# Where a step of layer 1's attention empties its accumulator bank: directly behind the value products, or at the end of the step

## The chip, the cores and the metric

The kernel runs on one core of one Trainium2 chip. The metric is device time in microseconds of one execution, taken as the median over runs. The engines carry their short names of the profile: PE is TensorE's matrix products (PEld its weight loads), DVE is VectorE, ACT is ScalarE, POOL is GpSimd, SP is SyncE, which issues the DMAs.

## What is computed

One inference step of a two-layer streaming encoder, over 2048 prompt frames and 64 sample frames of width 1024. Layer 0 has latent attention and banded attention. Layer 1, the one that matters here, is grouped-query attention in a sliding window: 16 query heads share 2 key/value heads of 64 dimensions, a chunk of 64 frames reads itself and the two chunks before it, and each head has a learned sink that joins the softmax's sum. The output is gated, projected and normalised:

```python
def _c_layer(h, pos, cache, pre_g, post_g, w_in, sinks, w_out):
    b, s, _ = h.shape
    xn = _rms(h, pre_g)
    q, k, v, g = _split(xn @ w_in, C_SIZES)
    ...
    if cache is None:
        o = _band_prompt(q, k, v, C_PAST_CHUNKS, C_SCALE, sinks=sinks)
    ...
    return h + _rms((o * jax.nn.silu(g)) @ w_out, post_g), state
```

## The kernel before

The kernel runs five phases one after the other. Phases 1 to 4 are layer 0 and the input projection of layer 1. Phase 5, which the change touches, is layer 1's attention together with its output projection, and it takes about the last 440 us. In all matrix products a number is split into a high and a low part, so a value operand has 128 columns: 64 of the high part and 64 of the low part.

**Units and blocks.** The prompt's 2048 queries are 16 blocks of 128, worked in the order 8 to 15, then 0 to 7 (`BLOCKS5`). A block has four units, one for each of two key/value heads `g` and each of two halves `e` of that head's query heads. A unit is four heads by 128 queries, against 256 keys in two tiles of 128. Block 0 has one tile of keys only (`nb` is 1), since nothing precedes it; it is the ninth block worked.

**Steps.** The loop over steps (`step`, line 1897) is a pipeline over units written out by hand. Step n exponentiates unit n+1 (line 1717, ACT), issues the scores of unit n+2 (line 1705, PE, with four row maxima on DVE, line 1708), turns the probabilities of unit n by transposes, and multiplies the turned probabilities of unit n-1, called `prv`, by its values. The last two go over the two key tiles, b = 0 and b = 1:

- `turn` (line 1723): four transposes into a bank `t` of PSUM (line 1726), and a copy of the high part into `PT` on ACT (line 211, a helper).
- `pump(RATE5 / 2)`: some products of the output projection of an older block (line 964). Now and then a half of a projected tile is finished; then ACT copies it to `z` (line 211) and squares it (line 983).
- `low()`: the low part of `PT`, on DVE (line 214, a helper), which reads the same bank `t`.
- at b = 0 only, `prv.av()` (line 1808): the value products of the previous unit, four matrix products (two for block 0) into the accumulator `acc`, line 1733.

**Evacuation.** After both tiles the step calls `prv.out()` (line 1813). ACT copies the low-part half of the accumulator to `tbm` (line 1822, shown as line 211), and DVE adds the other half to it and writes the block's output tile `OT` (line 1823). For the first unit of a block, (g, e) = (0, 0), `out` must first open a new `OT`. While two blocks are open it calls `J.rest()` and `pump(1)` until one of them is closed (lines 1816 to 1818). For the last unit, (1, 1), it also takes the reciprocal of the sums (line 1827) and hands the block to `gate`.

**Side work.** `J.rest()`, called at the end of every step and in that loop, moves several generators on by one stage. One is `gate` (line 1735): it spreads the reciprocals over the partitions by transposes (line 1755), multiplies `OT` by them on DVE (line 1757) and by the gate on POOL (line 1763), copies the result to `MM` on ACT (line 211), closes the block, and has POOL make the low part of `MM` (line 1770). Another is the tail of the output projection: a chain of small instructions for the root mean square, two multiplications `z` on DVE (line 995), the residual addition `x` on POOL (line 1003), and the store.

**Order.** From the ninth step on (`NAUTO5` is 8), PE, DVE, ACT and SP execute in the order in which the program names the instructions. POOL's order is left to the scheduler of the framework, and in the first eight steps so is that of all engines. Each engine works its queue in order.

**Space.** PSUM has 8 banks: two score tiles of two banks each, two banks `t` for transposes, one bank `acc` for value products, one bank `proj` for the projection. `OT` and `tbm` have two buffers each.

Of the kernel before, what the change touches and what calls it, by code (L numbers as in the profile page):

```python
# [110 lines left out]
def kernel(ctx, tc, a, o, upto=5):  # L111
# [1555 lines left out]
    def phase5():  # L1667

        with ExitStack() as st:
# [213 lines left out]
            def pump(rate):  # L1883
                if J.mm:
                    return J.pump(rate)
                for _ in range(RATEL):
                    if next(left, left) is left:
                        return open_projections()
# [8 lines left out]
            def step(n):  # L1897
                cur, prv, nxt = us.get(n), us.get(n - 1), us.get(n + 1)
                if nxt:
                    nxt.exp([0, 1, 2, 3])  # L1900
                if n + 2 < len(units):
                    us[n + 2] = Unit(*units[n + 2])
                    us[n + 2].start()
                    if n % 4 == 1 and n // 4 + 2 < 16:
                        blocks[n // 4 + 2] = Block(BLOCKS5[n // 4 + 2])
                for b in range(2):
                    low = None
                    if cur and b < cur.B.nb:
                        PT, low = cur.turn(b * 128, 128)
                        cur.tasks.append(PT)  # L1910
                    pump(RATE5 / 2)
                    if low:
                        low()
                    if b == 0 and prv:
                        prv.av()
                if prv:
                    prv.out()
                    us.pop(n - 1)
                    if n % 4 == 0 and n // 4 + 1 in blocks and n > 0:
                        blocks[n // 4 + 1].load_values()  # L1920
                if not J.loaded:
                    J.load.pump(1)
                if n >= NS5:
                    J.samp.pump(1)
                if J.made < FAST5:
                    J.side.pump(SP5)
                J.rest()

            for n in range(NAUTO5):
                step(n)  # L1930
            with manual(M5, ORDERED | {mybir.EngineType.SP}):
                for n in range(NAUTO5, len(units) + 1):
                    step(n)
                J.banks += [(ps_t, "t"), (ps_o, "acc")]
                J.dense = True
                while J.done < 17:
                    J.side.pump(TAIL)
                    J.samp.pump(1)
                    J.rest()
                    J.last = J.done == 16  # L1940
                    J.pump(4)
                J.side.drain()
                J.tails.drain()
# [104 lines left out]
```

## Time and profile before

| quantity | value |
|---|---|
| median of 3 runs | 2689.81 us (2688.68 to 2691.74) |
| the profiled execution, its own time | 2687.59 us |
| its span in the profile | 2685.8 us |
| granted TensorE clock, mean | 0.988 |
| PE busy | 2562.0 us (95%) |
| PEld busy | 2337.2 us (87%) |
| DVE busy | 1568.8 us (58%) |
| ACT busy | 1391.8 us (52%) |
| POOL busy | 520.5 us (19%) |
| DMA | 437.94 MB, mean 163 GB/s |

Times in the profile are microseconds from the start of the span. A row of a timeline gives the start, the time taken, the engine, the line of the kernel, the operation, the tile written and the tile read, their shapes and how many instructions the row merges. A bracket at its end gives the idle time of the engine just before and what ended it. The busy shares are means over the whole kernel; phase 5 has its own balance, which the prediction reads.

### The profile page before, as it was taken

Reading aid. Unit: us, or ns where it says so; the run is one execution under the profiler, and the core shown is the slowest. Engines: PE = TensorE matmul, PEld = TensorE weight load, DVE = VectorE, ACT = ScalarE, POOL = GpSimd, SP = SyncE. Lnnn points to the kernel's source line nnn. Section 1 sums busy time; section 2 is a strip of 40 time slices with the busy share of each in tenths; the row PEclk is TensorE's granted clock in tenths of the full one; section 3 lists DMA queues with packets and bytes.
Section 4 is the critical chain, followed back from the end, with each engine's and each line's share of the span. In section 5 each row is a group of like instructions: output and inputs, shape, how many; then the busy total and the mean of one; then the engine's idle time right before and its main releaser. Section 6 shows DMA issues by size and latency. Waiting matters only on the chain.

```text
span 2685.8 us, 46771 instructions
## 1 busy us (share of the span) xinstructions
PE 2562.0 (95%) x16296; PEld 2337.2 (87%) x16296; DVE 1568.8 (58%) x4299; ACT 1391.8 (52%) x3548; POOL 520.5 (19%) x1110
## 2 busy tenths in 40 slices
PE   7999999999999999999999999899999998999997
PEld 6999999899998888888778888689999998787886
DVE  6553345453227878787668776575224214787886
ACT  4332242322327777777667666553223214877773
POOL 0001000001002333221200323432001000344443
PEclk9999999999999999999999999999999999999999
DMA  7546343737537666661387776666525328555552
GB/s 243 170 152 210 124 149 113 246 111 220 173 94 201 190 180 185 175 188 49 114 243 188 201 201 177 176 233 230 152 84 176 122 72 249 118 142 135 132 133 71
DMA packets 382283, 437.94 MB, mean 163 GB/s; under 512 B 49936, under 2 KB 308888, under 8 KB 378816
## 3 DMA queue, kind: packets, MB, share of 16 engines
q1 hardware_dynamic: 382048, 434.95, 55.2%
q8 instruction: 130, 2.13, 0.3%
q14 instruction: 105, 0.86, 0.1%
HBM read 282.80 MB, written 157.09 MB: 164 GB/s over the span
## 4 chain that ended last, share of the span: by engine, by line
PE 79%; DVE 9%; ACT 5%; DMA 3%; issue 3%; POOL 1%; SPq 0%; ACTq 0%; DVEq 0%; POOLq 0%
PE pm L237 39%; PE proj L964 10%; PE s L683 6%; PE acc L754 4%; PE t L726 3%; PE acc L1228 3%; DVE PT L214 2%; PE s L1176 2%; PE t L1203 2%; PE t L1726 2%; PE acc L1733 2%; PE s L1705 1%; ACT P L702 1%; DVE m L689 1%; DVE s L1708 1%
## 5 line engine op out<-in xcount | busy, mean ns | idle before, releaser
L237 PE MATMUL pm<-X,W 128*128 128x384 f32 (+2 forms) x4536 | 754.3, 325 | 2.1 <-DVE ev L214 1.6
L237 PEld LDWEIGHTS pm<-X,W 128*128 128x128 f32 x4536 | 732.0, 189 | 5.3 <-DVE ev L214 1.9
L211 ACT ACTIVATE PT<-t 128x512 fp32r<-128x512 f32 (+3 forms) x704 | 344.1, 505 | 265.4 <-PE t L1203 76.2
L214 DVE SCALAR_TENSOR_TENSOR PT<-t,PT 128x512 fp32r<-128x512 f32 (+3 forms) x688 | 377.2, 569 | 91.6 <-ACT PT L211 89.0
L964 PE MATMUL proj<-Wo,MM 128*128 128x512 f32 (+1 forms) x1416 | 389.8, 406 | 5.0 <-ACT z L211 3.1
L214 DVE SCALAR_TENSOR_TENSOR ev<-pm,ev 128x256 fp32r<-128x256 f32 (+3 forms) x197 | 98.6, 503 | 336.0 <-ACT ev L430 101.2
L964 PEld LDWEIGHTS proj<-Wo,MM 128*128 128x128 f32 (+1 forms) x1416 | 245.2, 186 | 51.9 <-ACT z L211 6.5
L237 PE MATMUL pm<-W,X 128*128 128x256 f32 (+5 forms) x2040 | 281.2, 297 | 0.0
L237 PEld LDWEIGHTS pm<-W,X 128*128 128x128 f32 (+1 forms) x2040 | 272.0, 187 | 1.0
L702 ACT ACTIVATE P<-s,m 128x512 f32<-128x512 f32 (+9 forms) x344 | 209.5, 616 | 33.1 <-DVE m L691 30.5
L683 PE MATMUL s<-KA,Q 128*128 128x512 f32 (+7 forms) x640 | 201.4, 397 | 9.4 <-ACT P L702 8.4
L228 DVE TENSOR_TENSOR W<-R,W 128x768 fp32r<-128x768 f32 (+3 forms) x114 | 116.1, 1055 | 133.5 <-ACT W L227 133.1
L726 PE MATMUL t<-ident,P 128*128 128x128 f32 x1088 | 176.4, 276 | 3.4 <-ACT P L702 0.8
L689 DVE TENSOR_REDUCE m<-s 128x1 f32<-128x480 f32 (+7 forms) x216 | 132.4, 613 | 80.5 <-PE s L683 80.1
L726 PEld LDWEIGHTS t<-ident,P 128*128 128x128 f32 x1088 | 134.6, 141 | 41.6 <-ACT P L702 15.1
L754 PE MATMUL acc<-PT,V 128*128 128x256 f32 x1152 | 156.0, 285 | 6.5 <-DVE OT L763 6.5
L754 PEld LDWEIGHTS acc<-PT,V 128*128 128x128 f32 x1152 | 140.4, 188 | 12.0 <-PE t L726 6.0
L1717 ACT ACTIVATE P<-s,m 128x256 f32<-128x256 f32 (+2 forms) x264 | 119.6, 466 | 10.7 <-DVE m L1709 9.4
L1708 DVE CUSTOM_DVE_ANT_0 s<-s,mask 128x256 f32<-128x256 f32 (+1 forms) x256 | 107.6, 422 | 18.5 <-PE t L1726 7.7
L1228 PE MATMUL acc<-PT,V 128*128 128x256 f32 x672 | 111.5, 298 | 6.7 <-DVE OT L1238 4.5
L683 PE MATMUL s<-KR,Q 128*128 128x384 f32 (+6 forms) x320 | 116.3, 363 | 1.1 <-DMA Q<-sQR 1.1
L1180 DVE CUSTOM_DVE_ANT_0 s<-s,bias 128x640 f32<-128x640 f32 (+4 forms) x128 | 95.2, 744 | 35.1 <-PE s L1176 33.5
(251 smaller groups left out, 3941.2 us busy)
## 6 DMA issues: line engine op xcount, KB each, us to landing
Q<-sQA SPq DMA_DIRECT2D x128, 128.0 KB, 3.3
sWO<-W SPq DMA_DIRECT2D x32, 512.0 KB, 3.8
Q<-sQB SPq DMA_DIRECT2D x128, 128.0 KB, 3.3
Wo<-sWO SPq DMA_DIRECT2D x16, 1024.0 KB, 9.1
Q<-sQC SPq DMA_DIRECT2D x32, 512.0 KB, 7.2
R<-in_ab_w_in_dram SPq DMA_DIRECT2D x40, 384.0 KB, 4.0
K<-sKB SPq DMA_DIRECT2D x56, 256.0 KB, 5.4
V<-sVB SPq DMA_DIRECT2D x24, 512.0 KB, 6.3
```

What stands on the lines that cost most here:

```text
L211: nc.scalar.activation(out, in_, AF.Copy)
L214: nc.vector.scalar_tensor_tensor(out, x, scale, hi, op0=ALU.mult, op1=ALU.subtract)
L237: nc.tensor.matmul(ps, lhs(x, k), rhs(y, k), start=(j == 0), stop=(j == n - 1))
L683: nc.tensor.matmul(s[:r, :n], self.Q[:, x, self.qo:self.qo + r], rhs, start=(x == 0), stop=(x == 2))
L689: nc.vector.tensor_reduce(m[:r, j:j + 1], s[:r, :n], axis=AX.X, op=ALU.max)
L702: nc.scalar.activation(self.P[:r, o0:o0 + n], self.s.pop(j)[:r, :n], AF.Exp, bias=self.m[:r, 6:7], accum_out=acc)
L726: nc.tensor.transpose(t[:, b], self.P[:, (b0 + b) * 128:(b0 + b + 1) * 128], ident)
L754: nc.tensor.matmul(acc[:, (i // 2) % 2], H.V[:, b0 + b], PT[:, x, b], start=(b0 + b == 0 and x == 0), stop=(b0 + b == i and x == 1))
L964: nc.tensor.matmul(p, M[:, x, k, :r], W[k][:, y, cs], start=(k == k0 and t == 0), stop=(k == k1 - 1 and t == 2))
L1228: nc.tensor.matmul(acc, self.H.V[:, self.base - self.H.b0 + b], self.PT[:, x, off + b], start=(b == 0 and x == 0), stop=(b == nblk - 1 and ...
L1708: nc.vector.tensor_tensor_reduce(s[:, c, :w], s[:, c, :w], mk, 1.0, -3e38, ALU.add, ALU.max, m[:, 0, c:c + 1])
L1717: nc.scalar.activation(self.P[:, c, :w], self.s[:, c, :w], AF.Exp, bias=m[:, 1, c:c + 1], accum_out=m[:, 0, c:c + 1])
```

## The change

The call of `prv.out()` moves from behind the loop over the two key tiles into it, directly behind `prv.av()` at b = 0. With it move the copy to `tbm`, the addition, for a block's first unit the loop that runs side work and projection products until a block is closed, and for its last unit the reciprocal. What followed it in the step stays where it was.

```diff
                     if b == 0 and prv:
                         prv.av()
+                        prv.out()
                 if prv:
-                    prv.out()
                     us.pop(n - 1)
                     if n % 4 == 0 and n // 4 + 1 in blocks and n > 0:
                         blocks[n // 4 + 1].load_values()
```

## The prediction

> **What bounds the kernel now.** I read the page first, then the busy time by stretches, then the waits of the last 440 us (layer 1's attention with its output projection), then the timeline of single engines there.
>
> ```profile
> span 2685.8 us, 46771 instructions
> ```
>
> The busy time of two stretches follows. The columns are the stretch, its length, busy time of PE, PEld, DVE, ACT and POOL, granted clock, DMA share and GB/s.
>
> ```profile
> 2260.00:2300.00 40.00, 32.66 (x182) 23.42 (x181) 32.72 (x112) 30.48 (x99) 7.10 (x22) 0.96 0.64 177
> 2500.00:2550.00 50.00, 48.27 (x283) 40.98 (x283) 43.56 (x112) 39.64 (x118) 22.76 (x50) 1.00 0.57 139
> ```
>
> In the settled part TensorE is busy 48.27 of 50 us at full clock, VectorE 43.56. So TensorE sets the pace, and only its idle time, here 1.7 us in 50, can be won. The stretch from 2260 is looser: 7.3 us idle in 40. Who waits for whom from 2245 to the end (us in total, times, longest):
>
> ```profile
> DVE OT L1823 <- ACT tbm L211: 16.4, 28, 3.6
> PE acc L1733 <- DVE OT L1823: 13.9, 16, 3.8
> ```
>
> The value products wait 13.9 us for the addition that empties their only accumulator bank, by far TensorE's largest wait in this stage. TensorE's timeline shows where; the number in brackets is the idle time ahead of the row.
>
> ```profile
> 2363.72 1.17 PE L1733 MATMUL acc<-PT,VC 128*128 128x512 f32 x4 [0.58 <-DVE OT L1823]
> ...
> 2462.43 0.73 PE L1733 MATMUL acc<-PT,VC 128*128 128x512 f32 x2 [3.85 <-DVE OT L1823]
> ...
> 2607.49 1.16 PE L1733 MATMUL acc<-PT,VC 128*128 128x512 f32 x4 [0.71 <-DVE OT L1823]
> ...
> 2631.84 1.16 PE L1733 MATMUL acc<-PT,VC 128*128 128x512 f32 x4 [1.65 <-DVE OT L1823]
> ```
>
> From 2363.72 to 2607.49 there are ten such waits of 0.58 to 0.81 us, one in each block of four units (24.35 us apart when settled), together 7.2 us. Beside them stands one of 3.85, at the block that has a single tile of keys, and one of 1.65 at the end. The remaining 1.2 us lies in small ones, mostly before 2340, and I count nothing for it.
>
> Next, one settled block on four engines. I call three steps A, B and C. A's value products are those at 2399.74, and it evacuates the last unit of a block. B's are at 2405.27, and it evacuates the first unit of the next. C's are at 2412.39, and they stall.
>
> ```profile
> 2399.74 0.63 PE L1733 MATMUL acc<-PT,VC 128*128 128x512 f32 x2
> ...
> 2402.73 0.60 PE L1726 MATMUL t<-ident,P 128*128 128x128 f32 x4
> ...
> 2405.27 1.09 PE L1733 MATMUL acc<-PT,VC 128*128 128x512 f32 x4
> 2406.20 0.60 PE L1726 MATMUL t<-ident,P 128*128 128x128 f32 x4
> 2406.56 3.01 PE L964 MATMUL proj<-Wo,MM 128*128 128x512 f32 x12
> ...
> 2412.39 1.17 PE L1733 MATMUL acc<-PT,VC 128*128 128x512 f32 x4 [0.74 <-DVE OT L1823]
> ...
> 2415.07 0.66 PE L1726 MATMUL t<-ident,P 128*128 128x128 f32 x4
> ```
>
> ```profile
> 2400.84 0.60 ACT L211 ACTIVATE PT<-t 128x512 fp32r<-128x512 f32 x1 [2.11 <-PE t L1726]
> 2401.54 0.60 ACT L211 ACTIVATE z<-proj 128x512 f32<-128x512 f32 x1
> 2402.16 0.59 ACT L211 ACTIVATE tbm<-acc 64x512 f32<-64x512 f32 x1
> ...
> 2405.69 0.21 ACT L983 ACTIVATION_READ_ACCUMULATOR sq<-z 128x1 f32 x1
> 2406.84 0.60 ACT L211 ACTIVATE PT<-t 128x512 fp32r<-128x512 f32 x1 [0.93 <-PE t L1726]
> 2407.33 1.05 ACT L211 ACTIVATE MM<-OT 128x1024 fp32r<-128x1024 f32 x1
> 2408.41 0.60 ACT L211 ACTIVATE tbm<-acc 64x512 f32<-64x512 f32 x1
> ```
>
> ```profile
> 2402.79 0.68 DVE L1823 TENSOR_TENSOR OT<-acc,tbm 64x512 f32<-64x512 f32 x1 [0.62 <-ACT tbm L211]
> 2403.50 0.25 DVE L1827 RECIPROCAL ri<-rsum 128x16 f32<-128x16 f32 x1
> 2403.67 0.63 DVE L1757 TENSOR_TENSOR OT<-OT,t 128x512 f32<-128x512 f32 x1
> ...
> 2406.72 1.44 DVE L214 SCALAR_TENSOR_TENSOR PT<-t,PT 128x512 fp32r<-128x512 f32 x2
> 2408.08 3.57 DVE L995 SCALAR_TENSOR_TENSOR z<-z,rs,g_post 128x512 f32<-128x512 f32 x2
> 2411.57 0.68 DVE L1823 TENSOR_TENSOR OT<-acc,tbm 64x512 f32<-64x512 f32 x1
> ```
>
> ```profile
> 2404.38 2.40 POOL L1763 TENSOR_TENSOR OT<-OT,G 128x1024 f32<-128x1024 f32 x1 [4.17 <-DVE OT L1757]
> ...
> 2408.46 2.64 POOL L1770 TENSOR_TENSOR MM<-OT,MM 128x1024 fp32r<-128x1024 f32 x1 [1.37 <-ACT MM L211]
> ```
>
> A chain can be read off these rows. A's evacuation copy on ScalarE (tbm) stands behind a PT copy that waits for the second transposes, and behind a projection copy z, so it starts at 2402.16 although the products ended at 2399.74 + 0.63 = 2400.37. VectorE waits 0.62 us for it, then adds (OT), takes the reciprocal and does the gate's multiplication L1757. POOL waited 4.17 us for L1757. Its product L1763 is what ScalarE's MM copy reads, and POOL's MM subtraction waits for that copy. In B the program may not open a new OT buffer before the older block's MM is made (line 1816). So B's evacuation calls the side work, among it the MM copy and two z multiplications (L995), before its own two instructions. The second z ends at 2411.65, 0.55 us after the MM subtraction (2411.10). The addition follows, and 0.14 us after its end C's products start.
>
> **The change, part by part.** Nothing is added or removed. Each step's tbm copy and addition move ahead of the second PT copy (ScalarE) and the second low-part instruction, call it lo1 (VectorE). In B the side work and two small projection pumps move with them.
>
> *Step A.* tbm can run from 2400.4 to 2401.0, where ScalarE is idle (2.11 us). Queued behind this new wait are the second PT copy, z and the exponentials. The PT copy had to wait for transposes behind the same products, until 2400.84, and now starts at 2401.0: 0.16 us later, the price of the wait. The exponentials start 0.58 us sooner, since tbm no longer stands before them. On VectorE the addition runs 2401.0 to 2401.7 and the reciprocal to 2402.0; lo1 (0.72, half of the pair at 2406.72) ends at 2402.6, and L1757 runs 2402.6 to 2403.2 instead of 2403.67 to 2404.30: 1.1 us sooner. What lo1 reads, a transpose bank, comes free later, and the transposes at 2402.73 take that bank; the cover is 0.1 us, and without it about 0.1 us a block would be lost, 1 us in all. I count nothing.
>
> *Step B, engines other than TensorE.* L1763 ends at 2405.7 instead of 2406.78. ScalarE's work ahead of the MM copy ended at 2405.90 and now ends 0.58 sooner; the second PT copy, which waited until 2406.84, is no longer ahead. So the MM copy runs 2405.75 to 2406.8, 1.6 us sooner, and the MM subtraction 2406.9 to 2409.5. On VectorE the first low part runs 2405.6 to 2406.3, the first z to 2407.0, the second to 2409.5 + 0.55 = 2410.05, the addition (0.68) to 2410.7 and lo1 (0.72) to 2411.4. C's products need the addition and lo1, so they can start at 2411.55 by the same 0.14. TensorE would be there at 2412.39 - 0.74 = 2411.65. The stall goes, with only 0.1 us to spare. Next late are the transposes at 2415.07, which VectorE releases; it is 0.85 us sooner there and TensorE 0.74, so they get no worse.
>
> That the second z waits for POOL is read from its end and from a pair that took 1.40 us (below) against 3.57 here. The Trainium skill, page "SBUF — State Buffer", section "Who interferes with whom", says that a VectorE instruction with two SBUF inputs and a GpSimd instruction reading SBUF hold a port exclusively, and that whoever starts first blocks the other; the trace agrees with such a lock. If by that rule the second z got in first, POOL would start at 2407.75, lo1 would end near 2411.75, the gain would be 0.5 us a block, and the sum below 8 us instead of 10.5.
>
> *Step B, TensorE.* Six of the twelve products at 2406.56 (3.01 / 12 = 0.25 each, 1.5 us) now precede the second transposes, which end near 2408.3 instead of 2406.80. ScalarE's PT copy then ends near 2409.0, where tbm ended before (2409.01), and lo1's turn comes at 2410.7. So this is hidden, with 1.7 us of cover. The DMAs that the side work issues on SP's queue keep their order among themselves. C and the step after it have no side work ahead of the addition and only swap it with lo1, which costs nothing, since the next reader of either comes a step later.
>
> *The two odd places.* At the single-tile block VectorE and POOL show this:
>
> ```profile
> 2455.45 1.40 DVE L995 SCALAR_TENSOR_TENSOR z<-z,rs,g_post 128x512 f32<-128x512 f32 x2
> 2461.69 0.68 DVE L1823 TENSOR_TENSOR OT<-acc,tbm 64x512 f32<-64x512 f32 x1 [4.84 <-POOL MM L1770]
> ```
>
> ```profile
> 2456.93 2.37 POOL L1003 TENSOR_TENSOR x<-z,x 128x1024 f32<-128x1024 f32 x1 [1.72 <-DVE z L995]
> 2459.26 2.40 POOL L1770 TENSOR_TENSOR MM<-OT,MM 128x1024 fp32r<-128x1024 f32 x1
> ```
>
> Here POOL's queue holds the residual addition x ahead of the MM subtraction, and the OT addition waits for both. That step has no second tile, so its own order stays; only the step before it sends L1757 about 1.1 us sooner. I take 1.1, and at most 3.5 if x falls behind MM (2.37 more). At 2631.84 the chain is 0.85 us sooner, and I take 0.85. The end of the loop:
>
> ```profile
> 2640.81 1.08 PE L1733 MATMUL acc<-PT,VC 128*128 128x512 f32 x4
> ...
> 2644.66 0.73 PE L964 MATMUL acc<-Wo,MM 128*128 128x512 f32 x2 [1.65 <-DVE OT L1823]
> ```
>
> ```profile
> 2643.30 0.59 ACT L211 ACTIVATE tbm<-acc 64x512 f32<-64x512 f32 x1
> ```
>
> The last products end at 2641.89, and tbm stands behind a projection copy. It can start at 2641.95 instead of 2643.30. The next products wait 1.65 for it, so 1.3 us go, and the rest of the kernel hangs on that.
>
> **Sum:** 7.2 + 1.1 + 0.85 + 1.3 = 10.5 us. The profiled execution took 2687.59 us (span 2685.8); less 10.5 is 2677.1. The median of the runs shown is 2689.81, 2.2 higher, so I forecast 2679.3. The first eight steps are not in hand-written order; the scheduler may gain or lose up to the 7.3 us idle there. I take 0 and let a third count in the range.
>
> **Rivals.** *POOL's order flips (slower).* POOL's queue is not in hand-written order in this stage either. At the single-tile block, where no second tile precedes the z pair, x already stands ahead of MM and cost 3.85 us. The change puts every B into that shape. Then the z pair takes 1.40 and ends at 2407.7, x ends at 2410.1, MM at 2412.5, the addition at 2413.2, lo1 at 2413.95, and C starts at 2414.1 instead of 2412.39: 1.7 us lost in each of twelve blocks, 20 us, less 2.4 at the two odd places: near 2707. It decides when the second z is ready before the MM copy ends. Against it: the four row maxima of a full block are longer than those of the single-tile block, and by my times without any lock z would be ready near 2407.7, MM at 2406.8.
>
> *The wait changes hands (no difference).* lo1 now stands between the addition and C. If the MM chain moves only half of the 1.6 us, C waits for lo1 as long as it did for the addition: then only the odd places give, 2 to 3 us. If it doesn't move at all, 0.7 us a block is lost, net +5. For it: the margin is 0.1 us. Against it: both causes of the advance are plain in ScalarE's rows. The Trainium skill, page "Perfetto Trace Analysis", section "Optimization Strategy", reads one gap repeating on the busy engine as a sign of too few buffers; by that rule, with still one accumulator bank, this rival would hold.
>
> *The change doesn't act* in the scheduled steps: there its effect is drawn from the 7.3 us idle, either sign.
>
> **Numbers.** Forecast 0.60, changed hands 0.18, POOL's order 0.18, loss in the scheduled steps 0.04. A difference of 0.2% is 5.4 us, about what a measurement of this kernel can tell from no change. The forecast's own range is 2674 (10.5 + 2.4 for the odd block + 2.4 for the scheduled steps) to 2684. The range goes on to 2694, which is changed hands at its worst (+5), and leaves out POOL's order. Faster 0.59, same 0.20, slower 0.21.
>
> **What would show it.** Right: tbm starts within 0.1 us of the last value product in every step; L1757 in A about 1 us nearer to it; PE's wait for OT L1823 falls from 13.9 to under 5 us without a wait for PT in its place; blocks follow every 23.6 us; the MM subtraction still precedes x on POOL. Wrong: C stalls on DVE PT, or POOL lists x before MM in full blocks, or the stretch before 2300 grows.

## The result, and the profile after

| | median | runs | lowest to highest |
|---|---|---|---|
| before | 2690.37 us | 5 | 2688.68 to 2691.74 |
| after | 2673.93 us | 5 | 2665.11 to 2677.82 |

The changed kernel is faster by 16.4 us: a ratio of 0.9934 with an interval of 0.9915 to 0.9953. A second timing of the same kernel, in a later set of runs, gave 20.0 us (below). The forecast was 10.5 us less, so the direction and the mechanism held and the size did not: 2673.93 lies just under the low end of the range, 2674. One of the twelve executions of the kernel "first" below was slow, 4159.39 us at a granted clock of 0.557, and its ratio leaves it out.

The profile after is of an execution that took 2665.11 us, the shortest of its five. Its page begins, with PE's total behind it:

```profile
span 2663.3 us, 46751 instructions
...
PE 2549.5 (96%) x16296; PEld 2330.5 (88%) x16296; DVE 1568.7 (59%) x4299; ACT 1387.5 (52%) x3548; POOL 518.9 (19%) x1110
```

The span is 22.5 us shorter. TensorE's busy time fell too, by 12.5 us, with the same 16296 instructions. From the first product of line 1588, just ahead of layer 1's first scores, to the end of the span it fell from 412.24 to 406.17 us with 2338 instructions in both. That stretch is 20.3 us shorter, so 14.2 of it were shown as idle time of TensorE and 6.1 as busy time. That is the first hint of what the forecast missed.

The busy time of the two stretches that the prediction quoted, in the same columns:

```profile
2260.00:2300.00 40.00, 32.59 (x178) 22.63 (x179) 33.20 (x111) 29.70 (x98) 7.54 (x24) 0.96 0.59 161
2500.00:2550.00 50.00, 50.00 (x292) 43.03 (x291) 46.11 (x124) 41.77 (x127) 24.83 (x64) 1.00 0.59 148
```

In the settled part TensorE shows no idle time at all, where it was busy 48.27 of 50 us. In the stretch from 2260, which the scheduler orders, the idle time is what it was (32.59 busy against 32.66). One wait from 2225 to the end, again as total, times and longest:

```profile
PE acc L1733 <- DVE OT L1823: 2.6, 2, 2.4
```

The value products' wait for the addition fell from 13.9 us to 2.6. One block shows why. First A on ScalarE and VectorE, then B on ScalarE, VectorE and POOL, and last C's products on TensorE:

```profile
2394.36 0.59 ACT L211 ACTIVATE tbm<-acc 64x512 f32<-64x512 f32 x1 [1.76 <-PE acc L1733]
2394.98 0.60 ACT L211 ACTIVATE PT<-t 128x512 fp32r<-128x512 f32 x1
...
2399.60 1.06 ACT L211 ACTIVATE MM<-OT 128x1024 fp32r<-128x1024 f32 x1 [0.52 <-POOL OT L1763]
2400.69 0.59 ACT L211 ACTIVATE tbm<-acc 64x512 f32<-64x512 f32 x1
2402.11 0.60 ACT L211 ACTIVATE PT<-t 128x512 fp32r<-128x512 f32 x1 [0.82 <-PE t L1726]
```

```profile
2394.99 0.69 DVE L1823 TENSOR_TENSOR OT<-acc,tbm 64x512 f32<-64x512 f32 x1 [0.56 <-ACT tbm L211]
...
2395.86 0.63 DVE L214 SCALAR_TENSOR_TENSOR PT<-t,PT 128x512 fp32r<-128x512 f32 x1
2396.41 0.68 DVE L1757 TENSOR_TENSOR OT<-OT,t 128x512 f32<-128x512 f32 x1
...
2400.11 3.59 DVE L995 SCALAR_TENSOR_TENSOR z<-z,rs,g_post 128x512 f32<-128x512 f32 x2
2403.63 0.67 DVE L1823 TENSOR_TENSOR OT<-acc,tbm 64x512 f32<-64x512 f32 x1
2404.23 0.67 DVE L214 SCALAR_TENSOR_TENSOR PT<-t,PT 128x512 fp32r<-128x512 f32 x1
```

```profile
2397.16 2.41 POOL L1763 TENSOR_TENSOR OT<-OT,G 128x1024 f32<-128x1024 f32 x1 [3.05 <-DVE OT L1757]
...
2400.74 2.42 POOL L1770 TENSOR_TENSOR MM<-OT,MM 128x1024 fp32r<-128x1024 f32 x1 [0.86 <-ACT MM L211]
2403.78 2.41 POOL L1003 TENSOR_TENSOR x<-z,x 128x1024 f32<-128x1024 f32 x1 [0.62 <-DVE z L995]
```

```profile
2393.18 1.08 PE L1733 MATMUL acc<-PT,VC 128*128 128x512 f32 x4
...
2405.39 1.08 PE L1733 MATMUL acc<-PT,VC 128*128 128x512 f32 x4
```

A's products start at 2393.18 and C's at 2405.39. (In the prediction's block the row at 2399.74 is the last two of A's four products; the four start at 2399.29 and end at the same 2400.37.) In A, the evacuation copy (2394.36) and its addition (2394.99) are ahead of the second PT copy (2394.98) and the second low part (2395.86), and POOL's L1763 follows at once. In B the MM copy (2399.60) no longer stands behind a PT copy; that one comes at 2402.11 and has itself waited 0.82 for its transposes. POOL's subtraction ends at 2403.16, the z pair at 2403.70, lo1 at 2404.90, and C's products start at 2405.39 with no bracket. POOL still makes the subtraction before x. What is left is one block, the one with a single tile, where POOL still has x first:

```profile
2452.39 0.72 PE L1733 MATMUL acc<-PT,VC 128*128 128x512 f32 x2 [2.37 <-DVE OT L1823]
```

```profile
2446.91 2.39 POOL L1003 TENSOR_TENSOR x<-z,x 128x1024 f32<-128x1024 f32 x1 [1.71 <-DVE z L995]
2449.26 2.37 POOL L1770 TENSOR_TENSOR MM<-OT,MM 128x1024 fp32r<-128x1024 f32 x1
```

**Where the time went.** C's products, block after block, serve as marks; "a block" below is the time from C to C.

| stretch (of the two profiles) | before | after | saved |
|---|---|---|---|
| start to the first product of line 1588 | 2234.7 | 2232.5 | 2.2 |
| to the first mark (2363.72; 2359.17) | 129.0 | 126.7 | 2.3 |
| to the last mark (2607.49; 2588.88): eight ordinary blocks and the pair around the single tile | 243.77 | 229.71 | 14.06 |
| to the end of the span | 78.3 | 74.4 | 3.9 |

Eight ordinary blocks took 24.35 each and take 23.10. In the settled ones (24.35 and 23.11) 1.24 are saved, where the idle row said 0.72. The pair took 49.01 and takes 44.93. Of these 4.08 us, 1.72 lie ahead of the single-tile products, 1.57 between them and the next value products, and 0.79 behind. In the 1.57 it is the granted clock that differs (the column with 0.70 and 1.00), for the same 23 instructions, before and then after:

```profile
2462.43:2468.05 5.62, 5.62 (x23) 4.97 (x24) 5.28 (x20) 4.16 (x13) 1.52 (x9) 0.70 0.30 95
```

```profile
2452.39:2456.44 4.05, 4.05 (x23) 3.57 (x24) 3.81 (x14) 3.28 (x10) 0.69 (x4) 1.00 0.56 165
```

TensorE's rows around one C show what the idle row left out, before and then after:

```profile
2508.41 0.94 PE L964 MATMUL proj<-Wo,MM 128*128 128x512 f32 x3
2510.07 1.16 PE L1733 MATMUL acc<-PT,VC 128*128 128x512 f32 x4 [0.73 <-DVE OT L1823]
2511.07 0.60 PE L1726 MATMUL t<-ident,P 128*128 128x128 f32 x4
2511.43 1.19 PE L1705 MATMUL s<-KC,Q 128*128 128x256 f32 x8
2512.75 0.66 PE L1726 MATMUL t<-ident,P 128*128 128x128 f32 x4
```

```profile
2518.79 0.93 PE L964 MATMUL proj<-Wo,MM 128*128 128x512 f32 x3
2519.56 1.08 PE L1733 MATMUL acc<-PT,VC 128*128 128x512 f32 x4
2520.48 0.60 PE L1726 MATMUL t<-ident,P 128*128 128x128 f32 x4
2520.84 1.20 PE L1705 MATMUL s<-KC,Q 128*128 128x256 f32 x8
2521.92 0.66 PE L1726 MATMUL t<-ident,P 128*128 128x128 f32 x4
```

```profile
2512.75 0.42 PEld L1726 LDWEIGHTS t<-ident,P 128*128 128x128 f32 x4 [0.34 <-DVE PT L214]
```

From the start of the last projection products to C's products it is 1.66 us before and 0.77 after: 0.89 lost there, of which the bracket shows 0.73. The bracket counts from the end of the row in front, 2508.41 + 0.94 = 2509.35. Where nothing waits the next row starts before the recorded end of the row in front (2519.56 against 2518.79 + 0.93 = 2519.72), and these 0.16 us are missing from the bracket. From C's products to the next transposes it is 1.00 against 0.92, and from the scores to the transposes behind them 1.32 against 1.08. That last wait has no bracket on PE; the weight load's row has it, 0.34 for DVE PT. Together 0.89 + 0.08 + 0.24 = 1.21 of the 1.24.

### The profile page after: what moved, and what is told of

It reads as the page before. It is cut to its first block, busy times and chain, and to the rows that moved or that the text cites. A ratio compares the mean times of both kernels' runs of the same rounds, so it can differ in the third digit from the quotient of the medians.

```text
span 2663.3 us, 46751 instructions
## 1 busy us (share of the span) xinstructions
PE 2549.5 (96%) x16296; PEld 2330.5 (88%) x16296; DVE 1568.7 (59%) x4299; ACT 1387.5 (52%) x3548; POOL 518.9 (19%) x1110
## 4 chain that ended last, share of the span: by engine, by line
PE 80%; DVE 8%; DMA 5%; ACT 4%; issue 2%; POOL 1%; SPq 0%; ACTq 0%; DVEq 0%; POOLq 0%
PE pm L237 39%; PE proj L964 11%; PE s L683 6%; PE acc L754 4%; PE t L726 3%; PE acc L1228 3%; PE acc L1733 2%; PE t L1203 2%; PE s L1705 2%; PE t L1726 2%; PE s L1176 2%; DVE PT L214 2%; ACT P L702 1%; DVE m L689 1%; DMA R<-in_ab_w_in_dram 1%
```

## The experiments

The theory: C's products are held by a chain through both steps, from A's addition by way of POOL's L1763, the MM copy, POOL's subtraction and the z pair to B's addition. The rivals: one of the two steps does it alone; it is the evacuation itself (the bank free sooner) and not the place of the side work; the six projection products that now run ahead of B's transposes are what helps; POOL's order, left to the scheduler, is what matters. Each kernel's edit is shown against the changed kernel, and its times stand beside runs of the kernel before on the same chip.

**1. The changed kernel again.** No edit.

> The changed kernel once more, unaltered, as the measure for the others on this chip. Theory (the evacuations of a block's last and first unit together bring the MM subtraction forward, and the wait of the next value products goes): 14 to 20 us below the kernel before, blocks every 23.1 us, the single runs some us apart. Rival (the first five runs were a lucky spread and the phases ahead of layer 1 carry the excess over 10.5 us): 8 to 12 us below.

Measured 2671.12 (6 runs, 2666.99 to 2677.64) against 2691.15: ratio 0.9928 (0.9914 to 0.9941), 20.0 us. Its block is 23.13. From the first product of line 1588 to the end its profile takes 430.6 us, the first profile 430.8, the kernel before 451.1: some 20.4 us lie there. That product starts at 2236.3 here, later than in the kernel before, so the 2.2 us ahead of it in the first pair of profiles are spread between executions and not the change (from 1000 to 1500 the granted clock is 0.98 in the profile before and 0.99 in the first profile after).

**2. One kind of step at a time: last, first, middle.** The early call only for the block's last unit (step A), only for its first (step B), or only for the two between.

```diff
                         prv.av()
-                        prv.out()
+                        if (prv.g, prv.e) == (1, 1):
+                            prv.out()
                 if prv:
+                    if not ((prv.g, prv.e) == (1, 1)):
+                        prv.out()
```

(For "first" the pair is (0, 0), for "middle" the test is `prv.g != prv.e`.)

> Only the last unit of a block is evacuated directly behind its value products; the other three at the end of their step, as before. Theory: L1757 and POOL's L1763 come about 1 us sooner, but in the next step the PT copy still stands ahead of the MM copy and waits for its transposes, so the MM subtraction stays where it was and the wait at the third step stays near 0.7 us; only the single-tile block and the end gain, 2 to 4 us below the kernel before. Rival (every early evacuation brings its own share, four shares a block): about 4 us below as well. Rival (the six products that pass the transposes in the first unit's step are what helps): 0 to 3 us below.

> Only the first unit of a block is evacuated directly behind its value products, with its side work. Theory: the MM copy no longer stands behind the PT copy and comes 0.5 us sooner, but the low part that now follows the addition costs 0.7, so the wait grows by about 0.2 us a block: 0 to 4 us above the kernel before. Rival (four shares): about 4 us below. Rival (the six products ahead of the transposes): 10 us or more below.

> Only the second and third unit of a block are evacuated directly behind their value products. Theory: neither lies on the chain to the MM subtraction, so within 1.5 us of the kernel before, and the wait of 0.7 us a block stays. Rival (four shares): about 8 us below. Rival (six products): no difference.

| early in | median | ratio | block | TensorE's wait in a block |
|---|---|---|---|---|
| last | 2687.58 | 0.9986 (0.9977 to 0.9996) | 24.35 | at C, for OT |
| first | 2688.43 | 0.9991 (0.9981 to 1.0001) | 24.22 | at the transposes behind C, for PT |
| middle | 2691.69 | 0.9999 (0.9989 to 1.0008) | 24.36 | at C, for OT |

All stand beside 2691.15. The three bring 3.6, 2.7 and -0.5 us, 5.8 in all, of which only the first is clear of noise, and the change brings 20.0: A and B are worth little alone and much together. For "first" alone I had the sign wrong: it lost nothing. ScalarE and TensorE show why. "last" first:

```profile
2507.36 0.60 ACT L211 ACTIVATE PT<-t 128x512 fp32r<-128x512 f32 x1 [1.65 <-PE t L1726]
2507.86 1.05 ACT L211 ACTIVATE MM<-OT 128x1024 fp32r<-128x1024 f32 x1
```

```profile
2512.91 1.16 PE L1733 MATMUL acc<-PT,VC 128*128 128x512 f32 x4 [0.71 <-DVE OT L1823]
```

L1763 is done at 2506.20 there, but the MM copy stands behind the PT copy, which waits 1.65 us for B's second transposes, so the copy runs at 2507.86. In "first" it is the other way round:

```profile
2505.69 1.06 ACT L211 ACTIVATE MM<-OT 128x1024 fp32r<-128x1024 f32 x1 [0.92 <-POOL OT L1763]
...
2507.40 0.60 ACT L211 ACTIVATE PT<-t 128x512 fp32r<-128x512 f32 x1
```

```profile
2510.45 1.19 PE L1733 MATMUL acc<-PT,VC 128*128 128x512 f32 x4
...
2513.82 0.66 PE L1726 MATMUL t<-ident,P 128*128 128x128 f32 x4 [0.79 <-DVE PT L214]
```

Here the MM copy stands ahead of the PT copy and waits 0.92 for L1763, which comes as late as ever because A's addition does. What is won moves the wait from C's accumulator to the transposes behind it, 0.79 us. That is the second rival of the prediction, at another place: it happens when B alone is changed. A makes L1763 early, B lets the MM copy use it; each without the other runs into its own queue.

**3. The side work or the evacuation: lastloop.** A as in the change. In B only the loop that runs side work until a block is closed comes early; the copy and the addition stay at the step's end, in B and in the two steps between.

```diff
-                def out(self):
+                def open(self):
                     B, g, e = self.B, self.g, self.e
...
+                def out(self):
+                    B, g, e = self.B, self.g, self.e
                     tbm = sc.tile([64, 512], F32, name="tbm", bufs=2)
...
                         prv.av()
-                        prv.out()
+                        prv.open()
+                        if (prv.g, prv.e) == (1, 1):
+                            prv.out()
                 if prv:
+                    if (prv.g, prv.e) != (1, 1):
+                        prv.out()
```

> The last unit of a block is evacuated directly behind its value products; in the first unit's step only the side work and its two pumps move there, while the copy and the addition stay at the step's end; the other units as before. Theory (what counts in the first unit's step is that the MM copy no longer stands behind the second PT copy): blocks every 23.1 to 23.3 us, 16 to 20 us below the kernel before, as the changed kernel. Rival (the accumulator has to be emptied early in that step): the wait of 0.7 us a block stays, 3 to 5 us below.

Measured 2671.28 against 2690.42: 0.9928 (0.9913 to 0.9943), 19.1 us, with blocks of 23.20. By the medians that is the whole gain, and by the blocks all but 0.1 us of 1.24. So in B it is the place of the side work that counts, and the early evacuation brings next to nothing. In its profile, layer 1 takes 438.4 us against 430.8, but 4.6 of the 7.6 lie in the steps that the scheduler orders (granted clock 0.88 against 0.98 in the same steps) and 1.5 at the single-tile block (0.70 against 1.00). Whether the edit brings on these stretches of lower clock is not shown.

**4. The copy alone: actonly.** ScalarE's copy to `tbm` early in every step, the loop and the addition at the end.

```diff
                         prv.av()
-                        prv.out()
+                        prv.tbm = sc.tile([64, 512], F32, name="tbm", bufs=2)
+                        copy(prv.tbm, prv.acc[64:128])
                 if prv:
+                    prv.out()
```

(`out` then adds from this `tbm` and makes no copy of its own.)

> In every step the copy to tbm moves directly behind the value products, but the side work and the addition stay at the step's end. Theory: the MM copy still stands behind the second PT copy, so blocks stay at 24.3 us, and only the single-tile block and the end gain: 2 to 5 us below the kernel before. Rival (ScalarE's wait for the accumulator is what counted): 16 to 20 us below.

Measured 2688.80 against 2690.42: 0.9994 (0.9984 to 1.0005), blocks of 24.53. ScalarE's copy alone brings no gain, and the blocks are even 0.2 longer. As B's side work is late in this kernel too, it doesn't show by itself that the addition in A has to come early; that is argued from the chain, in which L1757 stands behind the addition.

**5. TensorE's order: peorder.** The changed kernel, but in B the second tile's transposes are issued ahead of the loop, so that the six projection products come behind them as before.

```diff
                         prv.av()
+                        if (prv.g, prv.e) == (0, 0) and cur and cur.B.nb > 1:
+                            t1 = cur.flip(128, 128)
                         prv.out()
```

(`flip` is the first half of `turn`, the four transposes; `turn` is handed `t1` and doesn't issue them again.)

> The changed kernel, but in the first unit's step the second tile's transposes are issued ahead of the six projection products of the side work, as TensorE had them before; the other engines keep the changed order. Theory: TensorE's order is neutral, 16 to 20 us below the kernel before, within 2 us of the changed kernel. Rival (the six products that pass the transposes fill a gap): at least 5 us above the changed kernel.

Measured 2674.46 against 2690.42: 0.9943 (0.9928 to 0.9958). Its blocks take 23.11 us, as in the changed kernel. The median is 3.3 above that of run 1, more than expected, but the two intervals overlap, and of its blocks only the pair around the single tile is longer in the profile (46.4 against 44.9). There the granted clock is 0.70 behind the wait of 2.37, as in the kernel before. The order on TensorE is not what brings the shorter blocks.

**6. The wait put back: delay.** The changed kernel with three needless additions of 64x256 on VectorE behind each block's first addition.

```diff
+                    if (g, e) == (0, 0):
+                        for _ in range(3):
+                            idle = sc.tile([64, 256], F32, name="idle", bufs=1)
+                            nc.vector.tensor_tensor(idle, self.acc[0:64, :256], tbm[:, :256], op=ALU.add)
```

> The changed kernel with three needless additions of 64 by 256 on VectorE behind each block's first addition (their result is not used), 1.1 to 1.2 us of VectorE. The changed kernel leaves 0.4 us between the low part's end and the next value products. Theory (a wait costs TensorE more than the idle time that its row shows, since the row counts from the modelled end of the product before): blocks 0.7 to 1.2 us longer than in the changed kernel, 8 to 14 us above it, and the idle time shown per block at least 0.2 us smaller than the lengthening. Rival (the shown idle time is the whole cost): lengthening and shown idle time agree within 0.1 us.

Measured 2690.05 against 2690.42: 0.9999 (0.9988 to 1.0009), some 19 us above run 1 and more than expected. Beside the blocks, the pair around the single tile is 4.5 us longer than in the changed kernel (49.46 against 44.93), with a wait of 3.69 there and a granted clock of 0.59 behind it. VectorE and TensorE in one block:

```profile
2516.22 1.31 DVE L1828 TENSOR_TENSOR idle<-acc,tbm 64x256 f32<-64x256 f32 x3
2517.45 0.67 DVE L214 SCALAR_TENSOR_TENSOR PT<-t,PT 128x512 fp32r<-128x512 f32 x1
```

```profile
2516.59 0.94 PE L964 MATMUL proj<-Wo,MM 128*128 128x512 f32 x3
2517.67 1.16 PE L1733 MATMUL acc<-PT,VC 128*128 128x512 f32 x4
2518.67 0.60 PE L1726 MATMUL t<-ident,P 128*128 128x128 f32 x4
2519.03 1.19 PE L1705 MATMUL s<-KC,Q 128*128 128x256 f32 x8
2520.95 0.66 PE L1726 MATMUL t<-ident,P 128*128 128x128 f32 x4 [0.73 <-DVE PT L214]
```

The additions hold VectorE 1.23 us (2516.22 to the start of lo1 at 2517.45), and the block takes 24.35 instead of 23.11: all of it is lost, so VectorE has no slack in this part of the changed kernel. What PE shows for it is 0.73. The rest is 0.31 between the projection products and C's products (1.08 against 0.77, without a bracket), 0.08 behind them, and 0.11 more at the transposes (1.92 from the scores against 1.08). The same 1.24 us a block, brought back by needless work, looks like 0.73 on the idle row.

**7. POOL's order written out: poolorder.** From the ninth step on POOL too goes in program order.

```diff
-            with manual(M5, ORDERED | {mybir.EngineType.SP}):
+            with manual(M5, ORDERED | {mybir.EngineType.SP, mybir.EngineType.Pool}):
```

> The changed kernel with POOL too in the order in which the program names its instructions from the ninth step on. That puts MM ahead of x at the single-tile block, and x ahead of MM at one full block near the beginning (the third subtraction). Theory: the wait of 2.4 us at the single-tile block goes, and at the block with x ahead one of 1.5 to 2.5 us appears, as the rival on POOL's order priced it (1.7 us against the kernel before, 2.4 for x itself): within 2 us of the changed kernel. Rival (POOL's order doesn't matter, the wait is elsewhere): neither wait changes.

Measured 2693.76 against 2690.45: 1.0013 (1.0002 to 1.0025), and the expectation of no difference to the changed kernel was wrong by about 22 us. Blocks take 25.00. POOL and then VectorE:

```profile
2512.64 0.20 POOL L1710 TENSOR_TENSOR m<-m,sink 128x4 f32<-128x4 f32 x1 [1.06 <-DVE m L1709]
2512.79 2.40 POOL L1763 TENSOR_TENSOR OT<-OT,G 128x1024 f32<-128x1024 f32 x1
2516.36 2.41 POOL L1770 TENSOR_TENSOR MM<-OT,MM 128x1024 fp32r<-128x1024 f32 x1 [1.18 <-ACT MM L211]
```

```profile
2509.71 0.68 DVE L1757 TENSOR_TENSOR OT<-OT,t 128x512 f32<-128x512 f32 x1
...
2518.81 0.68 DVE L1823 TENSOR_TENSOR OT<-acc,tbm 64x512 f32<-64x512 f32 x1 [2.41 <-POOL MM L1770]
```

L1757 has ended at 2510.39, but L1763 starts at 2512.79: a small addition to `m` (L1710) stands ahead of it in program order, and that one waits for VectorE's row maxima. The chain is 2.4 us later and the addition waits again, 2.41 us for the subtraction. So the gain needs L1763 not to stand behind that small addition, as the scheduler's order has it. It is not the pair that the prediction's first rival named (x and the subtraction), but the same queue. At the single-tile block the subtraction does come ahead of x here, and the wait there shrinks from 2.37 to 1.01.

**8. The odd block: oddfix.** At block 0 the loop calls the side work without the output's tails, so that POOL gets the subtraction before x.

```diff
-        def rest():
+        def rest(tails=True):
             J.load.pump(1)
             (J.side if J.side.q else J.samp).pump(1)
-            J.tails.each()
+            if tails:
+                J.tails.each()
...
                         while J.open >= 2:
-                            J.rest()
+                            J.rest(B.i > 0)
                             pump(1)
```

> The changed kernel, but at the single-tile block the loop that opens its output tile no longer moves the projection's tail on, so that POOL gets the MM subtraction ahead of the residual addition there. Theory (the 2.4 us wait left at that block is POOL's order): that wait shrinks below 0.5 us and the time is 2 to 3 us below the changed kernel. Rival (the wait is the copy on ScalarE or the multiplication ahead of it): no difference.

Measured 2669.56 against 2690.45: 0.9924 (0.9911 to 0.9936). The wait of 2.37 at the single-tile block is gone (the subtraction starts at 2446.02 and x 8 us later), and its profile's layer 1 takes 428.3 us against 430.8. So the cause of that wait is as the prediction read it. The medians cannot tell 2 us apart. The rows are POOL's:

```profile
2446.02 2.42 POOL L1771 TENSOR_TENSOR MM<-OT,MM 128x1024 fp32r<-128x1024 f32 x1 [0.87 <-ACT MM L211]
...
2454.17 2.39 POOL L1003 TENSOR_TENSOR x<-z,x 128x1024 f32<-128x1024 f32 x1 [1.49 <-DVE rs L187]
```

**9. The hand-written order earlier: early4.** As oddfix, with the hand-written order from the fifth step on instead of the ninth.

```diff
-NAUTO5 = 8
+NAUTO5 = 4
```

> The kernel of oddfix with hand-written order from the fifth step of layer 1's attention instead of the ninth. Theory (the idle 7 us of the first steps come from the scheduler's order): 1 to 4 us below oddfix. Rival (they come from the sample's attention and the transposes' two banks, whoever orders them): within 1.5 us of oddfix or slower.

Measured 2668.80 against 2690.45: 0.9924 (0.9912 to 0.9936). It can't be told from oddfix: 0.8 us below, where 1 to 4 were expected. The profiles don't settle it either: layer 1 takes 434.1 us here and 428.3 in oddfix, but the granted clock in its first 70 us or so is 0.86 here and 0.97 there. These two are the fastest versions here, and neither is told apart from the change itself.

## Why the prediction came out as it did

**What bounds the kernel.** Right. The waits named were the ones that went.

**Step A.** Right. In A, tbm starts 0.10 us after the products end (2393.18 + 1.08 = 2394.26; in B it comes 0.43 after them, behind the MM copy), L1757 runs 2.15 us after that end, where before it was 3.30 (2403.67 after 2400.37), so 1.15 sooner for the 1.1 worked out.

**Step B, engines other than TensorE.** Right in its order and nearly in its times. From the end of A's products to lo1's end it was to take 11.03 us and took 10.64. The subtraction took 2.42 and not the 2.64 of before, and the low part follows the addition 0.60 after its start, where I had added whole rows (0.68). The second z ended 0.54 us after the subtraction, as before (0.55). So VectorE did not get in first, and the Trainium skill's rule on the exclusive port (page "SBUF — State Buffer", section "Who interferes with whom") agrees with the pair's 3.59 us but decided nothing; the loss it allowed for did not come.

**Step B, TensorE.** Right: the products cost nothing, and neither did their order (run 5).

**The sum: this is the step that failed.** The ten waits, at about 0.72 each, were priced at 7.2 us; a block is 1.24 us shorter, about 11.2 us for the nine between the first mark and the last. I read the price of the stall from the brackets, and a bracket holds only part of it. The rest is the recorded end of the projection products in front, which the next row overlaps when nothing waits (0.16), the row behind (0.08), and the next transposes, of which the prediction said that they "get no worse" and which I counted at nothing (0.24). The weight load's bracket there, 0.34, would have shown that wait before the run, and the three intervals could have been compared with those of the other steps in the same block. Run 6 shows the same understatement from the other side. (The low end of the range is a little off too: 10.5 + 2.4 + 2.4 below 2689.81 is 2674.5, not 2674.)

**The single-tile block and the end.** Too small also. The pair saved 4.08, of which one ordinary block is 1.24, so 2.8 where I took 1.1. The bracket fell from 3.85 to 2.37, which is 1.48. The rest, some 1.4, goes with the clock, which the prediction put at nothing: 1.57 us were saved between the single-tile products and the next ones, where it was granted at 0.70 before and 1.00 after. The other profiles bear this out. Where the wait at that block is 3.69 or more (before, first, middle, delay), the clock behind it is 0.59 to 0.71; where it is 2.35 to 2.37, it is 0.70 in two (lastloop, peorder) and 1.00 in four (after, again, last, actonly); where it is 1.01 or none, it is 1.00 in all three. So the shorter wait made the stretch of lower clock rarer, but the profile after could have had it too, and that part is luck. At the end 3.9 were saved where I took 0.85 + 1.3 = 2.15. The 1.3 was right: from the last value products to the end it took 44.99 and takes 43.61. The 0.85 was not: from the last mark to the value products at 2631.84 (2611.06 after), where the whole bracket of 1.65 went, it took 24.35 and takes 22.18.

**The first steps.** Taken at nothing. From the first product of line 1588 to the first mark 2.3 us were saved, of which 0.58 was a bracket that I had counted. Up to the value products at 2331.84 (2329.35 after), which takes in all the steps that the scheduler orders, it is 0.3; the other 2.06 come in the hand-written steps, at the stall at 2338.53 (0.49), the transposes behind it, whose bracket falls from 1.10 to 0.37 (0.80), and the first mark (0.77).

**The rivals.** POOL's order did not flip in full blocks, and at the odd block it stood as before. That x ahead of the subtraction would cost 1.7 us in every block was not built as such; in run 7 it stands so once, with a wait of 3.11 at C. "The wait changes hands" came true only when B alone was changed (run 2). The Trainium skill (page "Perfetto Trace Analysis", section "Optimization Strategy") says that the same gap repeating on the engine that should be saturated can mean too little SBUF or PSUM for the next tile; here the gap of 0.7 us repeated in every block and went away with the same single accumulator bank, so an order of the queues was enough. A second bank was not tried.

**What stays open.** Single executions of one kernel differ by up to 14 us (after, 2665.11 to 2677.82; before, in the set of run 1, 2685.18 to 2699.02), and the gain was 16.4 in one set and 20.0 in the other. The granted clock goes with it in part: of the 69 runs of the kernel before in the three sets of the experiments, the 11 with a mean clock of 0.987 or less have a median of 2695.3, and the 12 with 0.991 or more one of 2688.8. What lowers the clock in one execution and not in another stays open, and so does what a second accumulator bank would bring.

## What to carry to other kernels

When a busy engine stalls at the same place in every round, take the price from the length of the round (the same stretch between the same rows, against a place where nothing waits), not from the idle time in the bracket, and look at the granted clock behind a long wait as well. A wait at the end of a chain through several in-order queues goes only when every place in which the chain stands behind something else is mended: here each of two steps alone brought some 3 us and both together 20. And an early place of an instruction matters by what it lets go behind it: in B the side work's place, not the evacuation, brought the gain.

## What the runs showed of the hardware that was not expected

The idle time ahead of a TensorE row understates a stall: 0.73 us shown for 1.24 of block length before, and again 0.73 for 1.24 when it was brought back with 1.23 us of needless VectorE work. Part of a wait is recorded as busy time of the products in front (0.16) and behind (0.08), and part has its bracket only in the row of the weight load (0.34). The granted clock behind a wait of 3.69 us or more was 0.59 to 0.71 in all four profiles that have one, and behind 2.35 to 2.37 us it was 0.70 in two of six and 1.00 in four; the same 23 instructions behind it took about 5.6 us at 0.70 and 4.05 at 1.00. The z pair took 3.59 us beside POOL's subtraction and 1.40 at the single-tile block, where POOL began only behind it; in both kernels the second z of a full block ended about 0.55 us after the subtraction.
